# A hybrid decoder step with 64 experts: the expert loop put into program order

## The chip, the cores and the metric

The kernel runs on one core of one Trainium2 chip. The metric is the device time of one execution in microseconds. The median of three runs of the kernel before is 1366.9 us (1366.76 to 1370.61).

## The reference

One layer of a decoder is run for 512 prompt tokens and 8 sample tokens, 520 rows of 1024 features, in float32. A state-space branch and a windowed attention branch are merged and normalised; then comes the part that the change touches, a mixture of 64 experts with 8 chosen for each token, a shared expert, and a gated input of the layer:

```
scores = sigmoid(x @ w_router)                       # (520, 64)
top 8 of scores + bias; gates = top_s / sum * 2.5
for each expert e, for its tokens:  acc[tok] += gate * (silu(x[tok] @ w1[e]) * (x[tok] @ w3[e])) @ w2[e]
shared = (silu(x @ ws1) * (x @ ws3)) @ ws2
ple    = sigmoid(x @ w_ple_gate) * (p @ w_ple)
y      = layer_norm(2**0.25 * x + acc + shared + ple)
```

w1 and w3 are 1024 x 256 for each expert, w2 is 256 x 1024.

## The kernel before, in words

**Numbers.** Every float32 operand of a large product is cut in two parts, `hi` (a rounded copy that ScalarE, ACT, writes) and `lo` (the rest, by a subtraction on VectorE, DVE, or GpSimd, POOL). TensorE (PE) then adds three products: hi by hi, lo by hi, hi by lo. `split` (line 267) issues both instructions. All weights are read from HBM as pieces of 128 x 1024 float32, 512 KB, and split on the chip.

**The stream of weights.** `Stream` (line 288) holds the list of pieces in the order in which they are used: for round e of the expert loop four pieces of w1 and w3 of expert e (A), then two pieces of w2 of expert e-1 (B). `get(n)` first splits up to two pieces beyond n. Five buffers hold split pieces; seven (at the start more) hold raw pieces. When a piece has been split, its raw buffer is free and the next load is given to the SyncE queue (SP). One split in six, that with `m % 6 == 2`, has its subtraction on POOL.

**The expert loop** (line 1599) has 65 rounds. The experts are sorted by their number of tokens, and `CAPS` gives the number of rows of each, from 112 to 56. Round e does:

- `expert_in(e)`: 24 matmuls of 512 columns with the turned rows of expert e, SiLU on ACT (line 1254), the product `hg` on DVE.
- `turn(e+1)`: eight transposes of the gathered rows `xg` of the next expert, in two PSUM banks, each split into `xgh` and `xgl`.
- `expert_out(e-1)`: 12 matmuls; ACT weighs the result with the gate into `y` (line 1450, two buffers), and POOL issues an indirect DMA that adds `y` to the rows of a sum in HBM (line 1451, the scatter). Two sums take turns up to expert 49, then all go to the first.
- `ffn_turn(e)`: two transposes of `hg`, split into `hh` and `hl`, which expert_out(e) needs in the next round.
- `fetch(e+3)`: the search for the rows of a later expert (`find`, line 1383): DVE compares places (`one_hot`), PE adds five small bf16 matmuls, DVE reduces them to `idx`; then POOL issues an indirect DMA that gathers the rows (line 1414), in three buffers.

**Side work** is spread over the rounds: the second half of the shared expert (`shared_more`), its output (`shared_out`), the layer input in four column groups (`layer_inputs`), the scales of the last norm, and the addition of the second sum to the rows (`second_sums`, on POOL). Each group begins with `side_weights`, which loads two or three pieces through one raw buffer and splits them in two to three splits at once. All side products use one PSUM buffer (`psx`), and so does the search from expert 3 on. Pieces are handed out by a quota, 44 over 55 rounds.

**The order.** Instructions are put in order by a scheduler of the framework, which estimates durations and may move an instruction ahead of others of its engine. `T.pinned` keeps PE's instructions in program order in the part before the loop and is False in the loop (line 1590); DVE, ACT and POOL are never pinned. On the chip each engine runs its instructions in the order so fixed, and waits at each for its data.

Of the kernel before, what the change touches and what calls it, by code (L numbers as in the profile page):

```python
# [18 lines left out]
F32 = mybir.dt.float32  # L19
# [9 lines left out]
NT = 520  # L29
# [18 lines left out]
YB = 2  # L48
PRE = 5
VB = 5  # L50
N_SIDE = 44
SECOND = 50
SIDE = N_SIDE / 55
N_DENSE = 54
assert len(CAPS) == NE

# [143 lines left out]
@with_exitstack  # L200
def trunk_step(ctx: ExitStack, tc: tile.TileContext, I, O):
    nc = tc.nc
    V, S, G = nc.vector, nc.scalar, nc.gpsimd

    class Tensor:

# [81 lines left out]
    class Stream:  # L288
# [34 lines left out]
        def split_to(self, n):  # L323
            while self.done < min(n, len(self.srcs)):
                p, tag, bufs = self.pools(self.done, 1)
                if p is None:
                    return
                self.load_to(self.done + 1)
                raw, was = self.raw.pop(self.done)
                hi = p.tile([128, 1024], F32R, tag=tag + "h", bufs=bufs, name="hi")  # L330
                lo = p.tile([128, 1024], F32R, tag=tag + "l", bufs=bufs, name="lo")
                m = self.done - P2 - 2
                split(hi, lo, raw, G if 0 < m < 6 * (NE - 1) and m % 6 == 2 else V)
                self.parts[self.done] = (hi, lo)
                self.done += 1
                self.held[was] -= 1
                self.load_to(self.done + 40)
# [957 lines left out]

    def shared_more(i):

        if i < 0:
            side_weights(lambda a, b: wd[50 + a // 1024], 2048)
            H['ph'], H['pl'] = (H[k][:, 0:2048].rearrange("p (k n) -> p k n", k=8) for k in ('ph', 'pl'))  # L1300
            return
        out = psx.tile([128, 512], F32, tag="x", name="x")[0:TT, 0:256]
        whole(shared_product(out, i, H['ph'], H['pl'], range(8)))
        shared_turn(shared_mid(out, moe.tile([MAX_CAP, 256], F32, tag="hg", bufs=2, name="sg")[0:TT, 0:128]), i, 1)

    def side_weights(src, n):

        H['ph'] = pw.tile([128, 2560], F32R, tag="ph", name="ph")
        H['pl'] = pw.tile([128, 2560], F32R, tag="pl", name="pl")
        for a in range(0, n, 1024):  # L1310
            b = min(a + 1024, n)
            raw = pw.tile([128, 1024], F32, tag="praw", name="praw")
            nc.sync.dma_start(raw[:, 0:b - a], src(a, b))
            split(H['ph'][:, a:b], H['pl'][:, a:b], raw[:, 0:b - a])

    def shared_out(i):

        if i < 0:
            side_weights(lambda a, b: wd[52 + a // 1024], 2048)
            H['ph'], H['pl'] = (H[k][:, 0:2048].rearrange("p (h k n) -> p h k n", h=2, k=2) for k in ('ph', 'pl'))  # L1320
            return
        hh, hl = H['shared'][:, i, 0], H['shared'][:, i, 1]
        for h in range(2):
            ps = psx.tile([128, 512], F32, tag="x", name="x")[0:TT]
            n = 0
            for k in range(2):
                for l, w in ((hh, H['ph']), (hh, H['pl']), (hl, H['ph'])):
                    T.matmul(ps, lhsT=l[:, k], rhs=w[:, h, k], start=(n == 0), stop=(n == 5))
                    n += 1
            v = H['x1'][:, i, 512 * h:512 * h + 512]  # L1330
            V.scalar_tensor_tensor(v, v, ALPHA, ps, op0=ALU.mult, op1=ALU.add)
        if i == 4:
            pT = py.tile([128, 2, NT], F32, tag="y", bufs=YB, name="pT")
            nc.sync.dma_start(pT, I['pT'])
            both = py.tile([128, 2, 2, NT], F32R, tag="side", name="pTs")
            H['pTh'], H['pTl'] = both[:, 0], both[:, 1]
            split(H['pTh'], H['pTl'], pT)

    def layer_inputs(q, i):

        if i < 0:
            side_weights(lambda a, b: I['wp'][q, :, a:b], 2560)
            H['ph'], H['pl'] = (H[k].rearrange("p (k n) -> p k n", k=10) for k in ('ph', 'pl'))
            return
        c = slice(TT * i, TT * i + TT)
        ps = psx.tile([128, 512], F32, tag="x", name="x")
        for o, xs, k0, kn in ((ps[0:TT, 256:512], (H['pTh'], H['pTl']), 0, 2), (ps[0:TT, 0:256], (H['xh'], H['xl']), 2, 8)):
            n = 0
            for k in range(kn):
                for l, w in ((xs[0], H['ph']), (xs[0], H['pl']), (xs[1], H['ph'])):  # L1350
# [20 lines left out]

    def second_sums(i):

        t = pw.tile([128, 1024], F32, tag="praw", name="second")[0:TT]
        nc.sync.dma_start(t, sumsD[1][TT * i:TT * i + TT])
        add(G, H['x1'][:, i], H['x1'][:, i], t)


    XG, XT, HG, HT, GC, IX = {}, {}, {}, {}, {}, {}

    OH = {}

    def find(e, what=(0, 1)):

        m = CAPS[e]
        if e not in OH:
            OH[e] = one_hot(e, m)
        a, b = what[0], what[-1] + 1
        ps = psx.tile([128, 512], F32, tag="x", name="x") if e > 2 else bank()
        for i in R5:  # L1390
            T.matmul(ps[0:m, 3 * a:3 * b], lhsT=OH[e][:, i], rhs=H['what'][:, i, 3 * a:3 * b, e], start=(i == 0), stop=(i == 4))
        both = moe.tile([128, 2], F32, tag="gc", bufs=8, name="both")
        V.tensor_reduce(both[0:m, a:b], ps[0:m, 3 * a:3 * b].rearrange("p (w n) -> p w n", n=3), axis=AX.X, op=ALU.add)
# [13 lines left out]

    def fetch(e):
        find(e)
        gather(e)  # L1410

    def gather(e):
        m = CAPS[e]
        G.indirect_dma_start(out=XG[e % 3][0:m], out_offset=None, in_=xD[:, :],  # L1414
                             in_offset=bass.IndirectOffsetOnAxis(ap=IX[e][0:m, 0:1], axis=0),
                             bounds_check=NT - 1, oob_is_err=False)

    def turn(e):
        x, m = XG[e % 3], CAPS[e]
# [17 lines left out]
    def expert_out(e):  # L1437
# [8 lines left out]
        if e >= NE - 2:  # L1446
# [4 lines left out]
        G.indirect_dma_start(out=sumsD[e % 2 if e < SECOND else 0][:, :], out_offset=bass.IndirectOffsetOnAxis(ap=IX.pop(e)[0:m, 0:1], axis=0),  # L1451
                             in_=y, in_offset=None, compute_op=ALU.add)

    def kept(e, ps):

# [21 lines left out]
    def second_phase():  # L1477
# [116 lines left out]
        fill(1000)  # L1594
        close_pool(disp)
        py = open_pool("py")
        side = [(q, i) for q in range(-2, 4) for i in range(-1, 5)]
        side += [(4, -1), (4, 0), (4, 1)] + [(5, i) for i in R5]
        for e in range(NE + 1):
            if e == NE - 1:  # L1600
                last_rows()
# [3 lines left out]
                turn(e + 1)  # L1605
            if e:
                expert_out(e - 1)
            else:
                H['shared'] = py.tile([128, 5, 2, 2, TT], F32R, tag="side", name="st")
                mids = py.tile([MAX_CAP, 1024], F32, tag="y", bufs=YB, name="mids")  # L1610
                mids = [shared_mid(H['first half'][i], mids[0:TT, 128 * i:128 * i + 128]) for i in R5]
            if 0 < e < 6:
                shared_turn(mids[e - 1], e - 1, 0)
            if 0 < e < NE - 1:
                HT[e] = ffn_turn(HG.pop(e), CAPS[e])
            if e + 3 < NE:
                fetch(e + 3)
            if e == 4:
                close_pool(pre)
                pw = open_pool("pw")  # L1620
            while side and (e - 4) * SIDE >= N_SIDE - len(side) + 1:
                q, i = side.pop(0)
                if q == -2:
                    shared_more(i)
                elif q == -1:
                    shared_out(i)
                elif q < 4:
                    layer_inputs(q, i)
                elif q == 5:
                    second_sums(i)  # L1630
                else:
                    last_scales(i)
        assert not side
        acc = {}
        for i in R5:
# [142 lines left out]
    def whole(g):  # L1778
        for _ in g:
            pass  # L1780
# [71 lines left out]
```

## Time and profile before

| | |
|---|---|
| median of 3 runs | 1366.9 us |
| profiled execution | 1371.03 us |
| its span, first to last instruction | 1369.2 us |
| mean granted clock of TensorE | 0.928 |
| PE busy | 1191.9 us, 87% |
| DVE busy | 970.3 us, 71% |
| ACT busy | 700.3 us, 51% |
| POOL busy | 560.2 us, 41% |
| HBM read and written | 276.32 MB and 32.87 MB |

The shares are of the span. Everything after this is read from stretches of the span, with times in microseconds from its start. A busy time of PE holds the modelled ends of its matmuls, which overlap. SiLU number e, the only instruction of line 1254, marks the end of expert_in(e), so the time between two of them is a round.

### The profile page before, as it was taken

To read this page: it belongs to the slowest core of one execution; us is meant where nothing else is said; L and a number is where in the kernel's file an instruction comes from. 1 tells how busy PE (TensorE), PEld (TensorE's weight loads), DVE (VectorE), ACT (ScalarE), POOL (GpSimd) and SP (SyncE) were. 2 spreads that over 40 slices of the span, in tenths; PEclk is the share of its full clock that TensorE was granted. 3 is DMA by queue.
4 is the path that set the end of the run, shared out by engine and by line. 5 is a ranking of instruction groups with operands and counts; after the bars stand their busy time and mean duration, and the time that the engine had idled before them with its cause. 6 is when DMAs were issued, how large, how long until landed. Compare 5 with 4: busy or idle time off the path is not lost. (4 is left out here: it accounts for less than half of the span.)

```text
span 1369.2 us, 20382 instructions
## 1 busy us (share of the span) xinstructions
PE 1191.9 (87%) x7082; PEld 890.2 (65%) x7084; DVE 970.3 (71%) x1397; ACT 700.3 (51%) x1055; POOL 560.2 (41%) x327
## 2 busy tenths in 40 slices
PE   7699899999997979787899688899999998968783
PEld 7699799999877756565566466576666664434441
DVE  7873748633588877576788578789789777647656
ACT  4131534222213766566567456767567665546562
POOL 1821231010124436243565354465664644464326
PEclk9898899999997989898999899999999999788896
DMA  7476553442512989798899798999999899887773
GB/s 286 134 240 120 191 182 105 118 116 92 191 60 89 294 222 314 226 286 262 257 319 319 224 274 275 310 306 305 303 300 321 288 301 266 224 229 243 260 191 100
DMA packets 114182, 312.93 MB, mean 229 GB/s; under 512 B 36986, under 2 KB 37410, under 8 KB 113000
## 3 DMA queue, kind: packets, MB, share of 16 engines
q1 hardware_dynamic: 68892, 249.24, 54.2%
q0 software_dynamic: 30208, 41.20, 14.0%
q10 hardware_dynamic: 14974, 21.14, 5.9%
q8 instruction: 57, 0.93, 0.3%
q14 instruction: 51, 0.42, 0.1%
HBM read 276.32 MB, written 32.87 MB: 226 GB/s over the span
## 5 line engine op out<-in xcount | busy, mean ns | idle before, releaser
L265 DVE TENSOR_TENSOR lo<-raw,hi 128x1024 fp32r<-128x1024 f32 x371 | 552.6, 1503 | 170.1 <-ACT hi L269 166.0
L269 ACT ACTIVATE hi<-raw 128x1024 fp32r<-128x1024 f32 x434 | 450.9, 1056 | 253.4 <-DMA raw<-in_we_dram 80.0
L1451 POOL DMA_INDIRECT accD<-y,idx x62 | 137.0, 2210 | 267.2 <-ACT hh L269 118.2
L210 PE MATMUL a<-hi,xgh 128*64 128x512 f32 (+18 forms) x512 | 211.8, 414 | 8.8 <-DVE xgl L265 6.0
L210 PE MATMUL a<-lo,xgh 128*64 128x512 f32 (+18 forms) x512 | 210.1, 410 | 7.3 <-DVE lo L265 7.3
L210 PE MATMUL a<-hi,xgl 128*64 128x512 f32 (+18 forms) x512 | 206.9, 404 | 0.0
L265 POOL TENSOR_TENSOR lo<-raw,hi 128x1024 fp32r<-128x1024 f32 x63 | 169.3, 2687 | 46.6 <-ACT hi L269 34.8
L1414 POOL DMA_INDIRECT xg<-xD,idx x64 | 125.0, 1953 | 146.5 <-DVE idx L1396 105.1
L210 PE MATMUL mm<-xh,hi 128*128 128x260 f32 (+1 forms) x576 | 121.7, 293 | 19.1 <-DVE r L259 10.7
L210 PE MATMUL mm<-xl,hi 128*128 128x260 f32 (+1 forms) x576 | 120.2, 291 | 0.8 <-DVE xl L265 0.8
L210 PE MATMUL mm<-xh,lo 128*128 128x260 f32 (+1 forms) x576 | 120.5, 291 | 0.0
L210 PEld LDWEIGHTS a<-hi,xgh 128*64 128x64 f32 (+18 forms) x512 | 75.7, 148 | 53.3 <-DVE xgl L265 7.6
L210 PEld LDWEIGHTS a<-lo,xgh 128*64 128x64 f32 (+18 forms) x512 | 75.6, 148 | 48.4 <-DVE lo L265 11.6
L210 PEld LDWEIGHTS mm<-xh,hi 128*128 128x128 f32 x576 | 92.8, 197 | 20.1 <-issue 11.0
L210 PE MATMUL mm<-lo,hh 128*64 128x512 f32 (+18 forms) x256 | 88.3, 428 | 18.3 <-POOL lo L265 17.8
L210 PEld LDWEIGHTS a<-hi,xgl 128*64 128x64 f32 (+18 forms) x512 | 75.5, 147 | 41.1 <-issue 4.0
L215 PE MATMUL a<-ident,xg 64*128 64x64 f32 (+18 forms) x512 | 57.7, 243 | 46.8 <-DMA xg<-xD,idx 38.5
L215 PEld LDWEIGHTS a<-ident,xg 64*128 64x128 f32 (+18 forms) x512 | 49.6, 148 | 73.0 <-DMA xg<-xD,idx 26.4
L210 PE MATMUL mm<-hi,hh 128*64 128x512 f32 (+18 forms) x256 | 88.0, 425 | 8.8 <-ACT hh L269 8.8
L1450 ACT ACTIVATE y<-mm,both 78x1024 f32<-78x1024 f32 (+19 forms) x62 | 68.8, 1109 | 52.1 <-PE mm L210 35.4
L210 PEld LDWEIGHTS mm<-xl,hi 128*128 128x128 f32 x576 | 92.2, 195 | 1.3 <-DVE xl L265 1.1
L210 PEld LDWEIGHTS mm<-xh,lo 128*128 128x128 f32 x576 | 92.4, 195 | 0.1
(410 smaller groups left out, 1999.1 us busy)
## 6 DMA issues: line engine op xcount, KB each, us to landing
raw<-in_we_dram SPq DMA_DIRECT2D x384, 512.0 KB
raw<-in_wd_dram SPq DMA_DIRECT2D x50, 512.0 KB
accD<-zeros_b POOLq DMA_DIRECT2D x2, 2560.0 KB
praw<-in_wp_dram SPq DMA_DIRECT2D x8, 512.0 KB
base<-in_xtok_dram ACTq DMA_DIRECT2D x1, 2080.0 KB
xD<-base ACTq DMA_DIRECT2D x5, 416.0 KB
second<-accD SPq DMA_DIRECT2D x5, 416.0 KB
acc<-accD SPq DMA_DIRECT2D x5, 416.0 KB
```

Of the source, the lines that this page charges most:

```text
L210: ins = nc.tensor.matmul(*a, **k)
L215: ins = nc.tensor.transpose(*a, **k)
L265: return e.tensor_tensor(out=o, in0=a, in1=b, op=ALU.subtract)
L269: a = S.activation(hi, src, AF.Copy)
L1414: G.indirect_dma_start(out=XG[e % 3][0:m], out_offset=None, in_=xD[:, :], in_offset=bass.IndirectOffsetOnAxis(ap=IX[e][0:m, 0:1], axis=0), ...
L1450: S.activation(y.rearrange("p (h n) -> p h n", h=2), ps[0:m], AF.Copy, scale=GC.pop(e)[0:m])
L1451: G.indirect_dma_start(out=sumsD[e % 2 if e < SECOND else 0][:, :], out_offset=bass.IndirectOffsetOnAxis(ap=IX.pop(e)[0:m, 0:1], axis=0), ...
```

## The change

In the expert loop the instructions of PE, DVE and ACT are marked to stay in program order, and so are gathers and scatters on POOL. `V` and `S` become wrappers that mark what they issue while `pinned` is True:

```diff
-    V, S, G = nc.vector, nc.scalar, nc.gpsimd
+    G = nc.gpsimd
+    class InOrder:
+        pinned = False
...
+            def run(*a, **k):
+                ins = call(*a, **k)
+                if self.pinned:
+                    tc.keep_in_program_order(ins)
+                return ins
+    V, S = InOrder(nc.vector), InOrder(nc.scalar)
```

All splits of weights have their subtraction on DVE, and the second sums are added there:

```diff
-                m = self.done - P2 - 2
-                split(hi, lo, raw, G if 0 < m < 6 * (NE - 1) and m % 6 == 2 else V)
+                split(hi, lo, raw)
...
-        add(G, H['x1'][:, i], H['x1'][:, i], t)
+        add(V, H['x1'][:, i], H['x1'][:, i], H['raw'])
```

The search takes a PSUM buffer of `psa2` (three, shared with expert_in, turn and the small transposes) for every expert:

```diff
-        ps = psx.tile([128, 512], F32, tag="x", name="x") if e > 2 else bank()
+        ps = bank()
```

The side work becomes a list of 55 pieces, each a load and a work. A weight split is a piece of its own. Each round from the fifth on does the work of one piece and then issues the load of the next:

```diff
+    def side_work():
+        groups = [(2, lambda c: wd[50 + c], shared_more), (2, lambda c: wd[52 + c], shared_out)]
+        for q in range(4):
+            groups.append((3, lambda c, q=q: I['wp'][q, :, 1024 * c:min(1024 * c + 1024, 2560)], lambda i, q=q: layer_inputs(q, i)))
+        for n, (parts, src, piece) in enumerate(groups):
+            for c in range(parts):
+                yield (lambda c=c, src=src: side_load(src(c))), (lambda c=c: side_weights(1024 * c))
+            for i in R5:
+                yield None, (lambda i=i, piece=piece: piece(i))
+            if n == 1:
+                yield side_tokens_load, side_tokens
+        for i in range(-1, 2):
+            yield None, (lambda i=i: last_scales(i))
+        for i in R5:
+            yield (lambda i=i: side_load(sumsD[1][TT * i:TT * i + TT])), (lambda i=i: second_sums(i))
```

`side_load` gives a load of 512 KB or less into the one raw buffer to SP; `side_weights` splits what it holds; `side_tokens_load` and `side_tokens` load and split the token features of the layer input, in one of the two `y` buffers. The loop becomes:

```diff
         for e in range(NE + 1):
...
                 turn(e + 1)
             if e:
                 expert_out(e - 1)
+            for n in (3, 4) if e == 0 else (e + 4,):
+                if n < NE:
+                    fetch(n)
+            if e - 1 in YE:
+                scatter(e - 1)
...
-            if 0 < e < NE - 1:
-                HT[e] = ffn_turn(HG.pop(e), CAPS[e])
-            if e + 3 < NE:
-                fetch(e + 3)
...
-            while side and (e - 4) * SIDE >= N_SIDE - len(side) + 1:
...
+            if e > 4 and side:
+                side.pop(0)[1]()
+            if e > 3 and side and side[0][0]:
+                side[0][0]()
+            if 0 < e < NE - 1:
+                HT[e] = ffn_turn(HG.pop(e), CAPS[e])
```

So the gather of a round is for expert e+4 instead of e+3 and stands ahead of the scatter on POOL, and ffn_turn stands behind the side piece.

## Rows read from the trace of the kernel before

**Rows 1.** Windows: us, busy time and count by engine, clock, DMA share, GB/s.
```profile
456.00:1343.00 887.00, 763.76 (x4059) 499.41 (x4057) 663.34 (x844) 551.65 (x764) 430.99 (x199) 0.93 0.89 272
860.00:980.00 120.00, 111.70 (x664) 77.81 (x663) 97.20 (x125) 81.21 (x113) 66.47 (x30) 0.98 0.97 307
```

**Rows 2.** Timeline: start, us, engine, line, tiles: SiLU 5, 60, 63; the closing matmuls.
```profile
521.87 0.38 ACT L1254 ACTIVATE hg<-a 92x256 f32<-92x256 f32 x1 [0.34 <-PE a L210]
...
1281.05 0.38 ACT L1254 ACTIVATE hg<-a 56x256 f32<-56x256 f32 x1 [0.67 <-PE a L210]
...
1328.10 0.38 ACT L1254 ACTIVATE hg<-a 56x256 f32<-56x256 f32 x1 [0.55 <-PE a L210]
...
1343.75 2.01 PE L210 MATMUL mm<-yy,to 128*104 128x512 f32 x4 [5.60 <-PEq L1645]
```

**Rows 3.** Waits of PE, 456 to 1343: us in total, times, longest.
```profile
PE a L215 <- DMA xg<-xD,idx: 38.1, 8, 9.7
```

**Rows 4.** Groups of splits, 456 to 1343: count, busy us, mean ns.
```profile
L265 DVE TENSOR_TENSOR lo<-raw,hi 128x1024 fp32r<-128x1024 f32 x318 | 479.8, 1524 | 113.2 <-ACT hi L269 109.2 <-issue 1.9
...
L265 POOL TENSOR_TENSOR lo<-raw,hi 128x1024 fp32r<-128x1024 f32 x62 | 166.9, 2692 | 46.5 <-ACT hi L269 34.8 <-issue 11.0
```

**Rows 5.** Timeline: splits on DVE with and without POOL beside them.
```profile
1234.31 3.49 DVE L265 TENSOR_TENSOR lo<-raw,hi 128x1024 fp32r<-128x1024 f32 x3
...
1238.67 2.42 POOL L262 TENSOR_TENSOR base<-base,second 104x1024 f32<-104x1024 f32 x1
...
1239.06 5.44 DVE L265 TENSOR_TENSOR lo<-raw,hi 128x1024 fp32r<-128x1024 f32 x1 [0.49 <-ACT hi L269]
```

**Rows 6.** Timeline: from the end of one expert_in to the split of the next rows.
```profile
1065.49 0.39 PE L210 MATMUL a<-hi,xgl 128*64 128x512 f32 x1
1065.72 0.61 PE L210 MATMUL mm<-hi,hh 128*66 128x512 f32 x2
1065.91 0.38 ACT L1254 ACTIVATE hg<-a 64x256 f32<-64x256 f32 x1 [3.66 <-PE a L210]
...
1066.26 0.71 PE L215 MATMUL a<-ident,xg 64*128 64x64 f32 x8
1066.33 0.41 DVE L259 TENSOR_TENSOR hg<-hg,a 64x256 f32<-64x256 f32 x1 [2.39 <-ACT hg L1254]
1067.23 0.64 ACT L269 ACTIVATE xgh<-a 128x256 fp32r<-128x256 f32 x2
```

**Rows 7.** Timeline: side matmuls, search, small transposes, one-hot, hi splits.
```profile
1039.89 0.28 PE L210 MATMUL x<-ph,x1h 128*104 128x256 f32 x1
...
1040.01 0.28 PE L210 MATMUL x<-pl,x1h 128*104 128x256 f32 x1
...
1046.49 0.33 PE L210 MATMUL x<-what,oh 104*64 104x6 bf16 x5
...
1046.74 0.34 PE L215 MATMUL a<-ident,hg 66*128 66x66 f32 x2
...
1046.89 0.42 PE L210 MATMUL a<-hi,xgh 128*66 128x512 f32 x1
...
1048.83 0.47 DVE L1404 TENSOR_TENSOR oh<-pc,place 104x320 bf16<-104x320 f32 x1
...
1058.35 3.90 ACT L269 ACTIVATE hi<-raw 128x1024 fp32r<-128x1024 f32 x4
```

**Rows 8.** Windows (columns as rows 1) behind two waits of PE.
```profile
1184.60:1191.30 6.70, 5.68 (x15) 3.04 (x16) 4.90 (x9) 3.22 (x4) 3.78 (x3) 0.50 0.98 284
1066.50:1073.00 6.50, 4.43 (x26) 2.60 (x25) 5.88 (x7) 4.81 (x8) 2.49 (x3) 1.00 0.72 179
```

**Rows 9.** Timeline: the wait of PE ahead of the first of those windows.
```profile
1184.62 0.47 PE L215 MATMUL a<-ident,hg 62*128 62x62 f32 x2 [1.26 <-DVE hg L259]
```

**Rows 10.** Tile y: the scatter on POOL (ns min/median/max), and its landing.
```profile
L1451 POOL DMA_INDIRECT accD<-y,idx x62: 1432/2014/4824, 471.9 to 1324.4; - x62
...
DMA to landing us min/median/max: 6.6/11.8/21.4
```

More of the change, by code (lines that the diff above doesn't have):

```diff
@@ L50 @@
 VB = 5
-N_SIDE = 44
 SECOND = 50
-SIDE = N_SIDE / 55
 N_DENSE = 54
@@ L202, in trunk_step, with __init__, __getattr__ @@
     nc = tc.nc
-    V, S, G = nc.vector, nc.scalar, nc.gpsimd
+    G = nc.gpsimd
+    class InOrder:
+        pinned = False
+        def __init__(self, engine):
+            self.engine = engine
+        def __getattr__(self, name):
+            call = getattr(self.engine, name)
+            def run(*a, **k):
[3 more added lines that the diff above has]
+                return ins
+            return run
+    V, S = InOrder(nc.vector), InOrder(nc.scalar)
     class Tensor:
@@ L1296, in shared_more, with side_load, side_weights @@
     def shared_more(i):
[L1298 to L1301, printed above, removed]
+        ph, pl = (t[:, 0:2048].rearrange("p (k n) -> p k n", k=8) for t in H['side'])
         out = psx.tile([128, 512], F32, tag="x", name="x")[0:TT, 0:256]
-        whole(shared_product(out, i, H['ph'], H['pl'], range(8)))
+        whole(shared_product(out, i, ph, pl, range(8)))
         shared_turn(shared_mid(out, moe.tile([MAX_CAP, 256], F32, tag="hg", bufs=2, name="sg")[0:TT, 0:128]), i, 1)
[L1306 to L1314, printed above, removed]
+    def side_load(src):
+        H['raw'] = pw.tile([128, 1024], F32, tag="praw", name="praw")[0:src.shape[0], 0:src.shape[1]]
+        nc.sync.dma_start(H['raw'], src)
+    def side_weights(a):
+        if a == 0:
+            H['side'] = [pw.tile([128, 2560], F32R, tag=nm, name=nm) for nm in ("ph", "pl")]
+        raw = H['raw']
+        split(*(t[:, a:a + raw.shape[1]] for t in H['side']), raw)
     def shared_out(i):
[L1318 to L1321, printed above, removed]
+        ph, pl = (t[:, 0:2048].rearrange("p (h k n) -> p h k n", h=2, k=2) for t in H['side'])
         hh, hl = H['shared'][:, i, 0], H['shared'][:, i, 1]
@@ L1326, in shared_out @@
             for k in range(2):
-                for l, w in ((hh, H['ph']), (hh, H['pl']), (hl, H['ph'])):
+                for l, w in ((hh, ph), (hh, pl), (hl, ph)):
                     T.matmul(ps, lhsT=l[:, k], rhs=w[:, h, k], start=(n == 0), stop=(n == 5))
@@ L1331, in shared_out, with side_tokens, side_tokens_load @@
             V.scalar_tensor_tensor(v, v, ALPHA, ps, op0=ALU.mult, op1=ALU.add)
[L1332 to L1337, printed above, removed]
+    def side_tokens():
+        both = py.tile([128, 2, 2, NT], F32R, tag="side", name="pTs")
+        H['pTh'], H['pTl'] = both[:, 0], both[:, 1]
+        split(H['pTh'], H['pTl'], H.pop('pT'))
+    def side_tokens_load():
+        H['pT'] = py.tile([128, 2, NT], F32, tag="y", bufs=YB, name="pT")
+        nc.sync.dma_start(H['pT'], I['pT'])
     def layer_inputs(q, i):
[L1341 to L1344, printed above, removed]
+        ph, pl = (t.rearrange("p (k n) -> p k n", k=10) for t in H['side'])
         c = slice(TT * i, TT * i + TT)
@@ L1349, in layer_inputs @@
             for k in range(kn):
-                for l, w in ((xs[0], H['ph']), (xs[0], H['pl']), (xs[1], H['ph'])):
+                for l, w in ((xs[0], ph), (xs[0], pl), (xs[1], ph)):
                     T.matmul(o, lhsT=l[:, k, c], rhs=w[:, k0 + k], start=(n == 0), stop=(n == 3 * kn - 1))
@@ L1372, in second_sums @@
     def second_sums(i):
-        t = pw.tile([128, 1024], F32, tag="praw", name="second")[0:TT]
-        nc.sync.dma_start(t, sumsD[1][TT * i:TT * i + TT])
-        add(G, H['x1'][:, i], H['x1'][:, i], t)
+        add(V, H['x1'][:, i], H['x1'][:, i], H['raw'])
[14 more added lines that the diff above has]
+            yield (lambda i=i: side_load(sumsD[1][TT * i:TT * i + TT])), (lambda i=i: second_sums(i))
     XG, XT, HG, HT, GC, IX = {}, {}, {}, {}, {}, {}
-    OH = {}
+    OH, YE = {}, {}
     def find(e, what=(0, 1)):
@@ L1409, in fetch @@
         find(e)
-        gather(e)
+        tc.keep_in_program_order(gather(e))
     def gather(e):
         m = CAPS[e]
-        G.indirect_dma_start(out=XG[e % 3][0:m], out_offset=None, in_=xD[:, :],
-                             in_offset=bass.IndirectOffsetOnAxis(ap=IX[e][0:m, 0:1], axis=0),
-                             bounds_check=NT - 1, oob_is_err=False)
+        return G.indirect_dma_start(out=XG[e % 3][0:m], out_offset=None, in_=xD[:, :],
+                                    in_offset=bass.IndirectOffsetOnAxis(ap=IX[e][0:m, 0:1], axis=0),
+                                    bounds_check=NT - 1, oob_is_err=False)
     def turn(e):
@@ L1450, in expert_out, with scatter @@
         S.activation(y.rearrange("p (h n) -> p h n", h=2), ps[0:m], AF.Copy, scale=GC.pop(e)[0:m])
-        G.indirect_dma_start(out=sumsD[e % 2 if e < SECOND else 0][:, :], out_offset=bass.IndirectOffsetOnAxis(ap=IX.pop(e)[0:m, 0:1], axis=0),
-                             in_=y, in_offset=None, compute_op=ALU.add)
+        YE[e] = y
+    def scatter(e):
+        y, m = YE.pop(e), CAPS[e]
+        sums = sumsD[e % 2 if e < SECOND else 0]
+        tc.keep_in_program_order(G.indirect_dma_start(
+            out=sums[:, :], out_offset=bass.IndirectOffsetOnAxis(ap=IX.pop(e)[0:m, 0:1], axis=0),
+            in_=y, in_offset=None, compute_op=ALU.add))
     def kept(e, ps):
@@ L1596, in second_phase @@
         py = open_pool("py")
-        side = [(q, i) for q in range(-2, 4) for i in range(-1, 5)]
-        side += [(4, -1), (4, 0), (4, 1)] + [(5, i) for i in R5]
+        side = list(side_work())
+        T.pinned = V.pinned = S.pinned = True
         for e in range(NE + 1):
@@ L1607, in second_phase @@
                 expert_out(e - 1)
-            else:
+            for n in (3, 4) if e == 0 else (e + 4,):
[3 more added lines that the diff above has]
+                scatter(e - 1)
+            if e == 0:
                 H['shared'] = py.tile([128, 5, 2, 2, TT], F32R, tag="side", name="st")
@@ L1620, in second_phase @@
                 pw = open_pool("pw")
-            while side and (e - 4) * SIDE >= N_SIDE - len(side) + 1:
[L1622 to L1632, printed above, removed]
+            if e > 4 and side:
[4 more added lines that the diff above has]
+                HT[e] = ffn_turn(HG.pop(e), CAPS[e])
+        T.pinned = V.pinned = S.pinned = False
         assert not side
```

## Prediction

> **What bounds the kernel now.** I read the windows first, then the waits, then the order of time inside single rounds. Everything that changes lies in the expert loop, from about 456 us to 1343.8 us, where the closing matmuls start [rows 1, 2]. There no engine is full: TensorE (PE) is busy 764 of 887 us at a mean granted clock of 0.93, VectorE (DVE) 663, ScalarE (ACT) 552, and the DMA engines 0.89 [rows 1]. The reader should see two loads near the length of the loop. The first is DMA: 887 us at 272 GB/s are 241 MB, and in the best long stretch (share 0.97) 307 GB/s flowed [rows 1], so these bytes need 786 us, 12.3 us in each of 64 rounds. The second is PE: 887 - 764 = 123 us idle, and a mean clock of 0.93 means about 124 us at the lower of its two levels, half of that lost, so that unbroken full-clock work would be some 710 us. Between 710 or 786 and 887 lies what order alone can win. The largest single wait of PE is for the gathered rows of an expert: 38.1 us in 8 waits [rows 3]. The gathers come late because POOL works in order, and a gather stands behind DVE splits given to POOL and behind scatters.
>
> **The change, part by part.**
>
> *Splits leave POOL.* 62 splits of 2.69 us go from POOL to DVE [rows 4]. On DVE three in a row took 3.49 us, 1.16 each [rows 5], so DVE gains 62 x 1.16 = 72 us. But DVE's 318 splits now average 1.524 us, because POOL's elementwise work stops DVE: one split took 5.44 us beside an addition of 2.42 us on POOL [rows 5]. Without that they lose 318 x 0.36 = 115 us. The five additions of second sums also go to DVE, the same width as a split, 5 x 1.16 = 6 us. DVE's load falls by about 37 us; nothing on the path is priced by it directly, since DVE is not full; what counts is its place in the round.
>
> *Program order: the round's timetable.* Program order decides who waits for whom, so I lay out one round with 0 at the moment when PE has issued the last matmul of expert_in. Matmuls of 512 columns follow each other by 0.23 us (1065.49 to 1065.72) [rows 6]: 24 of expert_in 5.55, 12 of expert_out 2.8. The eight transposes of turn take 0.71 [rows 6], the search 0.25 (1046.49 to 1046.74), the two transposes of ffn_turn 0.15 until the next matmul (1046.74 to 1046.89) [rows 7]; with the change of kind I take 0.2. PE alone would need 5.55 + 0.7 + 2.8 + 0.25 + 0.2 = 9.5.
> ACT: SiLU starts at 0.19 and ends at 0.57; xgh twice, 0.64 together, ends at 1.3 [rows 6]; then come the two hi splits of the next expert's first weights, 3.90/4 = 0.98 each [rows 7], ending at 2.3 and 3.3; then y.
> DVE: the product hg starts at 0.61 and takes 0.41 [rows 6]; the xgl halves lie before 2.3; the two lo splits end at 2.3 + 1.16 = 3.5 and 4.7; only then, since find stands behind expert_out in the program, comes the one-hot compare, 0.47 [rows 7], ending at 5.2.
> PE has issued turn and expert_out at 0.7 + 2.8 = 3.5 and the search needs the one-hot: a new wait of 1.7 us in each round with a search. The next expert_in starts at 5.2 + 0.25 + 0.2 = 5.65 and ends at 11.2; with hops between engines I take 11.3. DVE then splits from about 7 us on, four times 1.16, and ends near 11.7, in time for the next product at 11.9. Queued behind the waiting search on PE are the side piece, ffn_turn and the whole next expert_in; behind the one-hot on DVE the index for the gather. Bounds of this wait: 0, if the compare gets through early; 3 us, if it stands behind a split whose weights have not landed. I keep 1.7, the value of the rows.
> A piece of layer inputs is 30 matmuls of 256 columns at 0.12 (1039.89 to 1040.01) [rows 7], 3.5 us: such a round takes 14.8. A shared piece is 2.8 us of matmuls and about 1 us of waiting for SiLU and product, or for the one PSUM buffer: 15.1. The round of a weight split stays at 11.5, since its split stands in the gap and its data were asked for a round earlier.
>
> *The sum.* Rounds 5 to 59 carry 55 pieces: 20 x 14.8 = 296; 10 x 15.1 = 151; 16 weight rounds x 11.5 = 184; the token features 12; three pieces of scales and five second sums at 13, 104. Together 747 us, against 759 from SiLU 5 to SiLU 60 before [rows 2]. DMA does not set it: eight rounds of one layer-inputs group take 5 x 14.8 + 3 x 11.5 = 108 us, and DMA needs 8 x 12.3 = 98. The start, 66 us up to SiLU 5, I leave as it is: a gather wait goes, but the first rounds' order is stricter. The end, 62.7 us from SiLU 60, has no searches: three rounds at DMA's 12.3 and the 15.7 us from SiLU 63 on as now, 53 [rows 2]. So 66 + 747 + 53 = 866 before the clock. Before, the granted clock fell after a wait of 1.26 us and stayed at 0.50 for 6.7 us, but it held at 1.00 through 6.5 us of which PE was idle for 2.1 [rows 8, 9]. A fall of that length costs 3.35 us. The new waits are about as long as the first, the falls after long gather waits go, so I add four falls, 13 us: 879, against 887.8. That is 9 us less than the profiled execution's own 1371.0 (its span of 1369.2 and 1.8 around it); it ran 4.1 us above the median of 1366.9, so 1358 is the forecast for the median.
>
> *Smaller parts.* Gathers a round earlier and ahead of the scatter: the 38 us of waits [rows 3] go, and what is late next is the one-hot; this is in the timetable. The search in the banks of expert_in, turn and ffn_turn instead of the side buffer: it takes the bank that the product frees at 1.0, four microseconds before; nothing, and if DVE slipped by more than that, the wait would be the same as that for the one-hot. Side data loaded a round ahead: a load stands in SP's queue behind the weights and has a round of 11 us; nothing, at worst the wait of one landing in each of 22 loads, 2 us each. The token load takes one of two y buffers and waits for a scatter's landing, 11.8 us in the median [rows 10], about a round: 0 to 10 us once; I take 0.
>
> **Rivals.**
> A. DMA's pace. If the compare is early enough, the loop runs at the pace of the bytes: 786 us and some 20 for start and end, 806, 82 less: 1285. For it: 120 us at share 0.97 already now [rows 1]. Against: the timetable has DMA waiting in 30 of 55 rounds.
> B. Slower: the clock. The new wait comes in every round in the same place, between expert_out and the side piece or the next expert_in. If the clock falls in a quarter of the 55 rounds, 14 x 3.35 = 47 us instead of 13: 1392. It decides from seven falls on, (9 + 13)/3.35. For it: 0.50 after only 1.26 us; against: 1.00 through 2.1 us of idleness [rows 8, 9]. The Trainium skill (TensorE: Matmul & The Clock Gate, HAM oscillation) describes a loop that waits in each tile and falls back to the slow clock each time. By that all 55 rounds would fall, an estimate of 171 us more; the two gaps of the trace bear it out only in part.
> C. POOL and the scatters. From expert 50 on all scatters add into one buffer, each behind the last one's landing, 11.8 us in the median and 21.4 at most; POOL's part of a scatter goes from 1.4 to 4.8 us, 2.0 in the median [rows 10]; should DVE's added splits push each to the longest, 12 rounds with 2.8 more are 34 us: 1392. Against: the same chain stands there before. The Trainium skill (SBUF — State Buffer, Who interferes with whom) holds, as an inference, that a two-input vector operation does not keep GpSimd from writing descriptors. By that this rival costs nothing, and the spread of POOL's times would have another cause.
>
> **How the numbers follow.** The forecast has 0.60, with its own range of 1337 to 1375 (the wait in the search between 1.3 and 2.0 us). A has 0.10, B 0.22, C 0.08. A measurement here tells about 0.3%, 4 us, from no change. Of the forecast's 0.60 some 0.39 lie below 1362.8, 0.13 within, 0.08 above. Faster 0.39 + 0.10 = 0.49, same 0.13, slower 0.08 + 0.22 + 0.08 = 0.38. The range reaches past B and C and more than halfway to A: 1314 to 1398.
>
> **What would show it.** Right: PE's largest wait in the loop is that of the search's weight load for the one-hot, some 55 times about 1.7 us; hardly a wait for gathered rows; splits on DVE at 1.2 us; rounds of 11 and 15 us. Wrong: no such wait and DMA at 0.97 (A); a clock under 0.9 through the middle of the loop (B); gaps at y or at the gathers after expert 50 (C).

## The result: 4% slower, and the profile after

The changed kernel takes 1425.2 us (median, 1419.8 to 1434.1) against 1368.7 for the kernel before on the same chip: ratio 1.0419, 95% interval [1.0355, 1.0484]. The forecast was 1358, its range ended at 1398. The profiled execution took 1419.8 us with a span of 1418.0 and a mean granted clock of 0.922.

The loop's milestones, from the timeline of the kernel after (start, us, engine, line, tiles; SiLU 5, 60 and 63, then the closing matmuls, as in [rows 2]):

```profile
522.66 0.38 ACT L214 ACTIVATE hg<-a 92x256 f32<-92x256 f32 x1 [1.68 <-PE a L228]
...
1333.90 0.38 ACT L214 ACTIVATE hg<-a 56x256 f32<-56x256 f32 x1 [2.28 <-PE a L228]
...
1377.05 0.38 ACT L214 ACTIVATE hg<-a 56x256 f32<-56x256 f32 x1 [1.43 <-PE a L228]
...
1390.52 0.72 PE L228 MATMUL last<-yy,to 128*104 128x512 f32 x1 [5.15 <-PEq L1676]
```

SiLU 5 to SiLU 60 took 811.2 us, before 759.2. SiLU 5 came 0.8 us later, and from SiLU 60 to the closing matmuls it took 56.6 us instead of 62.7. So the loss lies in rounds 5 to 59. Three stretches of them by the windows (columns as in [rows 1]): all of them, 6.7 us around a late compare, and the best long one:

```profile
522.66:1333.90 811.24, 679.13 (x3601) 447.58 (x3599) 553.36 (x799) 471.91 (x658) 184.67 (x110) 0.92 0.84 264
566.30:573.00 6.70, 3.84 (x21) 3.84 (x22) 2.10 (x4) 2.04 (x2) 1.75 (x2) 0.50 0.64 195
924.90:1028.50 103.60, 91.29 (x551) 62.53 (x549) 78.12 (x117) 67.80 (x96) 28.52 (x16) 1.00 0.90 288
```

The DMA engines were less busy (0.84; 0.91 before in the same rounds), DVE and POOL had more room than before. Nobody is full; everybody waits. The waits, by engine (who waits for whom: us in total, times, longest), whole span:

```profile
PE a L228 <- DVE oh L214: 121.1, 62, 6.6
PE a L228 <- ACT hi L214: 18.0, 3, 9.3
...
ACT hi L214 <- DMA raw<-in_we_dram: 47.9, 43, 3.4
ACT y L214 <- DMA accD<-y,idx: 41.7, 7, 11.0
...
SPq L336 <- DVE lo L214: 782.5, 356, 25.2
```

PE's wait for gathered rows, 38.1 us in [rows 3], has vanished; the search's wait for the one-hot compare stands in its place, three times as large. The groups of instructions that answer to [rows 4] (count, busy us, mean ns, then the idle time before them):

```profile
L214 DVE TENSOR_TENSOR lo<-raw,hi 128x1024 fp32r<-128x1024 f32 x434 | 519.6, 1240 | 136.0 <-ACT hi L214 128.9 <-DMA raw<-in_we_dram 5.7
...
L1443 POOL DMA_INDIRECT xg<-xD,idx x64 | 82.4, 1288 | 638.9 <-issue 485.3 <-PE a L233 118.4 <-DVE oh L214 17.6
```

Splits went from a mean of 1.52 to 1.24 us, as forecast. A gather's issue holds POOL for 1.29 us in the mean (1.95 before).

What a bad round is made of shows in the timeline of the kernel after at three places: an ordinary late compare (903 to 906 us), a very late one (566 to 569), and a late y (519 to 540):

```profile
519.66 2.38 POOL L1485 DMA_INDIRECT accD<-y,idx  x1 [0.30 <-DVE lo L214]
...
536.68 1.11 ACT L214 ACTIVATE y<-mm,both 94x1024 f32<-94x1024 f32 x1 [11.00 <-DMA accD<-y,idx]
...
538.98 3.90 ACT L214 ACTIVATE hi<-raw 128x1024 fp32r<-128x1024 f32 x4
...
540.09 0.73 PE L228 MATMUL a<-hi,xgh 128*88 128x512 f32 x1 [7.14 <-ACT hi L214]
...
566.28 1.06 ACT L214 ACTIVATE hi<-raw 128x1024 fp32r<-128x1024 f32 x1 [1.79 <-DMA raw<-in_we_dram]
...
567.37 1.23 DVE L214 TENSOR_TENSOR lo<-raw,hi 128x1024 fp32r<-128x1024 f32 x1 [1.62 <-ACT hi L214]
568.51 0.59 DVE L214 TENSOR_TENSOR oh<-pc,place 104x420 bf16<-104x420 f32 x1
569.16 0.53 PE L228 MATMUL a<-what,oh 104*84 104x6 bf16 x5 [6.63 <-DVE oh L214]
...
902.77 1.21 DVE L214 TENSOR_TENSOR lo<-raw,hi 128x1024 fp32r<-128x1024 f32 x1
903.22 1.06 ACT L214 ACTIVATE hi<-raw 128x1024 fp32r<-128x1024 f32 x1 [0.88 <-DMA raw<-in_we_dram]
...
904.31 1.22 DVE L214 TENSOR_TENSOR lo<-raw,hi 128x1024 fp32r<-128x1024 f32 x1 [0.33 <-ACT hi L214]
905.45 0.52 DVE L214 TENSOR_TENSOR oh<-pc,place 104x350 bf16<-104x350 f32 x1
906.02 0.34 PE L228 MATMUL a<-what,oh 104*70 104x6 bf16 x5 [3.03 <-DVE oh L214]
```

At 902.77 and 904.31 DVE makes the two splits, and only then the compare, which depends on neither. The second split waits for ACT, ACT for weights that land 0.88 us late: the compare, the search, and on PE all that stands behind the search are late with them. At 566 the weights land later still and PE stands for 6.6 us; at 536 ACT holds four splits behind y, which has no buffer until a scatter issued 17 us earlier has landed.

### The profile page after: what moved, and what is told of

It is laid out like the page before. It is cut to its first block, busy times and chain, and to the rows that moved or that the text cites. A ratio compares the mean times of both kernels' runs of the same rounds, so it can differ in the third digit from the quotient of the medians.

```text
span 1418.0 us, 20397 instructions
## 1 busy us (share of the span) xinstructions
PE 1204.1 (85%) x7083; PEld 900.3 (63%) x7084; DVE 943.1 (67%) x1465; ACT 694.5 (49%) x1055; POOL 342.9 (24%) x259
## 3 DMA queue, kind: packets, MB, share of 16 engines
q1 hardware_dynamic: 68892, 249.24, 51.2%
q0 software_dynamic: 30208, 41.20, 13.6%
## 5 line engine op out<-in xcount | busy, mean ns | idle before, releaser
L214 DVE TENSOR_TENSOR lo<-raw,hi 128x1024 fp32r<-128x1024 f32 x434 | 519.6, 1240 | 136.0 <-ACT hi L214 128.9
L214 ACT ACTIVATE hi<-raw 128x1024 fp32r<-128x1024 f32 x434 | 435.6, 1056 | 175.7 <-PE mm L228 54.4
L1443 POOL DMA_INDIRECT xg<-xD,idx x64 | 82.4, 1288 | 638.9 <-issue 485.3
L228 PE MATMUL a<-hi,xgh 128*64 128x512 f32 (+18 forms) x512 | 218.2, 426 | 18.1 <-ACT hi L214 18.0
L228 PE MATMUL a<-hi,xgl 128*64 128x512 f32 (+18 forms) x512 | 213.2, 416 | 0.0
L1485 POOL DMA_INDIRECT accD<-y,idx x62 | 128.8, 2077 | 94.4 <-DMA accD<-y,idx 26.4
L228 PE MATMUL mm<-xh,hi 128*128 128x260 f32 (+1 forms) x576 | 121.2, 292 | 22.4 <-DVE r L214 12.5
L228 PE MATMUL a<-what,oh 104*64 104x6 bf16 (+18 forms) x335 | 24.2, 186 | 122.0 <-DVE oh L214 121.1
L228 PEld LDWEIGHTS <-oh 104*64 104x64 bf16 (+18 forms) x345 | 19.3, 122 | 152.2 <-DVE oh L214 149.6
L228 PE MATMUL mm<-lo,hh 128*64 128x512 f32 (+18 forms) x256 | 80.2, 394 | 1.7 <-DVE lo L214 1.7
L228 PE MATMUL mm<-hi,hl 128*64 128x512 f32 (+18 forms) x256 | 79.8, 393 | 0.0
```

The costliest lines, as they stand in the source:

```text
L214: ins = call(*a, **k)
L228: ins = nc.tensor.matmul(*a, **k)
L1443: return G.indirect_dma_start(out=XG[e % 3][0:m], out_offset=None, in_=xD[:, :], in_offset=bass.IndirectOffsetOnAxis(ap=IX[e][0:m, 0:1], a ...
L1485: tc.keep_in_program_order(G.indirect_dma_start(out=sums[:, :], out_offset=bass.IndirectOffsetOnAxis(ap=IX.pop(e)[0:m, 0:1], axis=0), in_= ...
```

## An account of the rounds

For each kernel I split the time from SiLU 5 to SiLU 60 into three: PE's idle time ahead of its instructions; what the half clock cost (half of the half-clock time in which PE was not idle); and the rest, PE's work at full clock. All are worked out from the profiled execution.

| kernel | SiLU 5 to 60 | PE idle | half-clock loss | rest | median, ratio to before [95%] |
|---|---|---|---|---|---|
| before | 759.2 | 95.3 | 29.8 | 634.0 | 1366.9 |
| after | 811.2 | 132.1 | 51.2 | 627.9 | 1425.2, 1.042 [1.036, 1.048] |
| e1 compare early | 764.1 | 92.5 | 32.5 | 639.0 | 1376.3, 1.009 [1.005, 1.012] |
| e2 shared turns early | 806.8 | 128.7 | 51.2 | 626.9 | 1419.6, 1.041 [1.033, 1.048] |
| e7 e1 and e2 | 758.5 | 90.5 | 30.0 | 637.9 | 1361.2, 0.997 [0.994, 1.000] |
| e13 e7, splits 3 ahead | 755.1 | 89.0 | 33.7 | 632.3 | 1357.2, 0.997 [0.994, 1.000] |
| e15 e13, compare first | 749.1 | 84.1 | 31.5 | 633.6 | 1349.3, 0.990 [0.985, 0.995] |
| e3 PE, POOL in order | 782.5 | 107.1 | 49.3 | 626.1 | 1401.8, 1.027 [1.017, 1.037] |
| e6 DVE, ACT, POOL in order | 824.1 | 123.1 | 70.7 | 630.4 | 1438.4, 1.052 [1.046, 1.057] |
| e4 no order | 727.9 | 69.1 | 23.5 | 635.3 | 1327.0, 0.973 [0.966, 0.980] |
| e10 e4, shared bank | 736.4 | 77.0 | 29.0 | 630.4 | 1351.6, 0.993 [0.991, 0.995] |
| e11 e4, old place of fetch | 752.0 | 102.6 | 20.7 | 628.7 | 1358.7, 0.996 [0.993, 0.999] |
| e14 e4, splits on POOL | 748.7 | 80.7 | 32.3 | 635.6 | 1364.5, 1.000 [0.997, 1.004] |
| e5 before, splits on DVE | 804.0 | 127.2 | 47.7 | 629.1 | 1410.0, 1.032 [1.025, 1.039] |
| e16 before, gather early, own bank | 746.0 | 84.6 | 26.7 | 634.7 | 1364.4, 1.000 [0.997, 1.003] |

The rest is 626 to 639 us in all kernels. No version does less work; they differ in how long PE stands still and in what the half clock costs.

## Experiments: is it the compare, or landings and buffers?

**e1: the compare made early, all else in program order.**
```
                 turn(e + 1)
+            if 0 < e and e + 4 < NE:
+                OH[e + 4] = one_hot(e + 4, CAPS[e + 4])
             if e:
                 expert_out(e - 1)
```


> Theory 1 (the compare): in program order the one-hot compare stands on DVE behind two splits of the next expert's weights, so PE waits at the search in every round, 121 us in all, longer where the weights land late, and the clock falls behind the long ones. With the compare issued right behind the turned rows that wait goes and rounds of layer inputs fall from 14.5 to about 13 us: 1425 becomes 1320 to 1360. Theory 2 (landings): the rounds are set by the landing of weights and scatters, and the compare is only where PE shows it. Then PE's wait moves to the hi and lo splits, and the time stays above 1400.

Measured 1376.3 us: 49 us of the 56 lost come back with one instruction moved. PE's largest waits in e1, 456 to 1345 us:

```profile
PE a L228 <- ACT hi L214: 49.9, 20, 8.4
PE a L228 <- DVE lo L214: 31.4, 38, 2.1
```

The wait for the compare in the loop is down from 120.0 to 6.0 us, but half of it has become waits for the next splits: what the compare hid behind itself. The compare is the larger cause, not the only one; the time falls between the two ranges.

**e2: all five turns of the first shared half in round 1**, so that their buffer, one of the two of y, is free from then on.
```
-            if 0 < e < 6:
-                shared_turn(mids[e - 1], e - 1, 0)
+            if e == 1:
+                for i in R5:
+                    shared_turn(mids[i], i, 0)
```


> The five products of the first shared half hold one of the two y buffers up to round 5, so y waits 11 us there for a scatter's landing, with all of ACT's later splits behind it. Here all five are turned in round 1 and the buffer is free from then on. Theory 1: 11 us and the round behind it are won, 1405 to 1415; the search waits stay near 120 us. Theory 2 (landings): the late weights of rounds 7 to 11 come from this stop, so those rounds get shorter too, 1385 to 1405.

Measured 1419.6, only 5.6 less and above both ranges; the intervals overlap. SiLU 5 to 6 fell from 23.6 to 12.0 us, but rounds 7, 8 and 11 still take 21.6, 19.7 and 19.4 with the compare late as before (122.2 us of waits, 62 times).

**e7: both edits.**

> The changed kernel, all in program order, with the compare of round e + 4 moved to just behind the turn of round e + 1 (1376 alone) and the five turns of the first shared half all in round 1 (1420 alone). If the two losses are separate and add: 1376 less 5.6 = 1368 to 1373. If the wait for y's buffer in round 5 was covered by the late compare and shows once that is gone: 1355 to 1367.

Measured 1361.2, in the second range, 15 us below e1: once the compare is early, y's wait is on the path. From 456 to 545 us y waits 19.5 us for scatters in e1 and 1.9 in e7, and SiLU 5 comes at 509.4 instead of 527.4 us, so most of this gain lies ahead of the stretch in the table. The changes don't add; one wait covered the other.

**e13: e7, and each weight block split three blocks ahead of its matmuls instead of two** (`def get(self, n, ahead=3)`).

> The changed kernel in program order with the compare early and the shared turns all in round 1 (1361), and each weight block split three blocks ahead of its matmuls instead of two. Theory J (what is left of the loss against 1327, 34 us, comes of splits just in time: they free the raw buffers late, loads start late, and TensorE waits 73 us for hi and lo): 1335 to 1350. Theory Q (a third split between product and compare only moves the wait, ACT and DVE stand in order behind a landing in either case): 1356 to 1375.

Measured 1357.2 (in the profile, 33 us of PE's waits are for the compare again: the third split stands ahead of it). Theory Q's range holds, and so does its mechanism.

**e15: e13, with the compare ahead of all splits of its round.**
```
+            if 0 < e and e + 4 < NE:
+                OH[e + 4] = one_hot(e + 4, CAPS[e + 4])
             if 0 < e < NE:
                 expert_in(e)
```


> The changed kernel in program order, shared turns in round 1, splits three blocks ahead (1357), and the compare of round e + 4 ahead of all splits of round e. Theory H (the rest of the order's loss is still the compare behind a split, 32 us of TensorE's idle time): 1325 to 1340. Theory W (the rest is weights that land late, with the splits and all that stands behind them in order): 1345 to 1360, the wait for the compare gone and that for hi grown.

Measured 1349.3, the best in program order, inside theory W's range. The waits of e15:

```profile
PE a L228 <- ACT hi L214: 34.7, 12, 9.4
PE a L228 <- DVE lo L214: 24.8, 30, 2.6
...
ACT hi L214 <- DMA raw<-in_we_dram: 102.7, 68, 5.4
...
ACT y L214 <- DMA accD<-y,idx: 44.9, 7, 12.3
```

The compare is gone from the list (3.6 us in all). What stays is splits whose weights have not landed, and y behind scatters, with all later splits of ACT behind it.

## Experiments: whose order costs?

**e4: nothing held in program order**, gathers and scatters included; side work, early gathers, own bank and splits as in the change.
```
-        T.pinned = V.pinned = S.pinned = True
+        pass
...
-        tc.keep_in_program_order(gather(e))
+        gather(e)
...
-        tc.keep_in_program_order(G.indirect_dma_start(
+        G.indirect_dma_start(
...
```


> No engine is in program order in the loop; all other parts of the change stay (splits on DVE alone, one side piece a round loaded a round ahead, the search in the shared banks, gather four ahead). If program order is the whole loss (theories 1 and 2 alike), the time is that of before or less, 1330 to 1375. If the other parts cost (DVE's 72 us of added splits, three banks for everything), it stays above 1390.

Measured 1327.0, below both ranges: program order costs 98 us, and the other parts of the change gain 40 against the kernel before. From 767 to 1263 us of e4 (windows):

```profile
767.00:1263.00 496.00, 458.48 (x2512) 293.23 (x2509) 369.23 (x541) 327.40 (x453) 138.92 (x76) 0.97 0.94 296
```

In the kernel after DMA flowed at 272 GB/s there. The timeline of e4 in one round shows the other order:

```profile
890.05 0.31 PE L228 MATMUL a<-what,oh 104*68 104x6 bf16 x5
...
891.06 0.50 DVE L214 TENSOR_TENSOR oh<-pc,place 104x340 bf16<-104x340 f32 x1
```

The search of one expert runs unhindered, and the compare after it is for a later one, placed between two splits.

**e3 and e6: one side of the order each.** e3 keeps PE and the gathers and scatters in order (`T.pinned = True` alone), e6 keeps DVE, ACT, gathers and scatters (`V.pinned = S.pinned = True`).

> Only PE, gathers and scatters keep program order in the loop; DVE and ACT are free for the scheduler again. Theory 1: the scheduler can put compare and product ahead of splits, the search wait falls below 40 us and the time to 1340 to 1390. Theory 2: the rounds stay as long, 1410 to 1430.

> The changed kernel with TensorE taken out of the program order; DVE, ACT and the gathers and scatters keep it. Theory C (the loss is made in DVE's and ACT's order: the one-hot compare behind two splits, y's scaling ahead of later splits; TensorE then only passes it on): 1390 to 1420 us, since the compare still comes as late as before, though TensorE may run a shared piece in that time. Theory P (TensorE's fixed order is what turns late operands into idle time): with other matmuls to run while the compare is late, 1330 to 1360.

e3 took 1401.8, between its ranges, and e6 1438.4: each alone is slow, and e6 came out 13 us above all four in order (1.052 against 1.042, intervals that just overlap). e3 lost the wait for the compare and got others; that DVE now serves its queue in another order than PE's is the likely reason, not shown by itself. The waits of e3 and of e6:

```profile
PE a L228 <- DVE hg L214: 29.6, 14, 6.0
PE a L233 <- DVE xgl L214: 20.6, 12, 4.4
PE a L233 <- DVE st L214: 18.7, 2, 9.5
PE a L233 <- DVE hl L214: 18.6, 7, 9.5
```

```profile
PE a L228 <- DVE oh L214: 88.7, 46, 5.5
```

So theory C holds for e6, beyond its range: with DVE and ACT fixed, a free PE still waits 88.7 us for the compare, and it stood at half clock for 150 us of rounds 5 to 59. That a part's cost is this engine's or that one's can't be said; orders must fit each other.

## Experiments: where do the 40 us come from?

**e5: the kernel before, its POOL splits on DVE** (`split(hi, lo, raw)` for the line that chose POOL).

> The kernel before with one edit: the 63 splits that ran on POOL run on DVE, all else as it was, in the scheduler's order. Theory S (the gain of some 40 us that the changed kernel keeps with nothing held in program order, 1327 against 1367, comes from POOL's splits alone: DVE's splits lose the neighbour that stretches them, 1.52 to 1.24 us in the mean): 1325 to 1340 us. Theory R (it comes from the rest: the work spread a piece a round and loaded a round ahead, the search in a bank of its own, the place of the gathers and scatters): 1355 to 1375, the split mean down to 1.3 us all the same.

Measured 1410.0: this part of the change alone is a loss of 43 us. The split's mean is 1.25 us, as hoped, but the view of waits of e5 shows the price:

```profile
PE a L215 <- DMA xg<-xD,idx: 87.4, 17, 13.5
```

It was 38.5 in the whole span before. Both theories fall. On POOL, where gathers and scatters take turns, the scatter now waits 242.9 us for ACT's y, 27 times (72.4 and 12 before), and a gather lands 12.5 us after its issue in the median instead of 8.8. Gathers stand behind that scatter in POOL's order; what lengthens the landing no run shows.

**e11: e4 with the search and gather at their old place**, expert e + 3 behind the scatter and the shared turn, instead of e + 4 ahead of them.
```
-            for n in (3, 4) if e == 0 else (e + 4,):
-                if n < NE:
-                    fetch(n)
...
+            if e + 3 < NE:
+                fetch(e + 3)
```


> The changed kernel with nothing held in program order (1327), but the search and gather of expert e + 3 behind the scatter and the shared turn of round e, as in the kernel before, instead of expert e + 4 ahead of that scatter. Theory F (the lead of the gather is the gain over 1410): 1370 to 1400, with waits for gathered rows of 50 us or more. Theory K (own bank) or spread side work: 1325 to 1340, the gathers in time all the same.

**e10: e4 with the search in the side work's single PSUM buffer again** (`ps = psx.tile(...) if e > 2 else bank()`).

> The changed kernel with nothing held in program order (1327), and the search from expert 3 on again in the side work's single PSUM buffer, as in the kernel before. That kernel with all splits on DVE takes 1410, 87 of its idle microseconds waiting for gathered rows. Theory K (the own bank is what lets the search and so the gather come early): 1380 to 1410, with TensorE waiting for gathered rows 60 us or more. Theory F (the gain lies in where the gather is issued and in the side work spread a piece a round): 1320 to 1335.

e11 took 1358.7, e10 1351.6: 32 and 25 us lost. The waits for gathered rows, first e11, then e10:

```profile
PE a L233 <- DMA xg<-xD,idx: 102.1, 20, 18.4
```

```profile
PE a L233 <- DMA xg<-xD,idx: 17.5, 5, 7.1
```

The gather's place is worth most, by the mechanism that theory F named (its range was too high); the bank is worth nearly as much, between the two ranges, and only a part of that is in the gather's wait.

**e14: e4 with the splits back on POOL. e16: the kernel before with the gather's new place and the own bank, splits still on POOL.**

> The changed kernel with nothing held in program order (1327) and the 63 splits back on POOL, as in the kernel before. Theory M (the move itself was a loss, hidden behind the earlier gather): 1290 to 1318 us. Theory N (the move costs only where it makes gathers late; beside it POOL's elementwise work stretches DVE's splits from 1.24 to 1.5 us): 1327 to 1345.

> The kernel before, splits on POOL and in the scheduler's order, with two things of the change: the search in the bank of expert_in and turn, and search and gather of expert e + 4 ahead of the scatter. If these two are the whole gain of the changed kernel without program order: 1320 to 1332 us, waits for gathered rows under 10 us. If the side work a piece a round and loaded ahead carries a part: 1335 to 1355.

1364.5 and 1364.4, both no different from before and above every range that I gave. The wait for gathered rows is under 1 us in both. In e14 PE waits for POOL's own splits instead, 42.6 us where it was 17.8 before; in e16 that wait stays at 16.7, and PE's idle time is spread over many others, 84.6 us between SiLU 5 and 60 against 95.3. The waits of e14:

```profile
PE mm L228 <- POOL lo L283: 42.6, 19, 7.3
```

This gives three corners of a square: splits moved alone, +43; gather early and own bank alone, 0; both, with the spread side work and the second sums on DVE, -40. With splits on POOL these last two make no difference (e14 against e16); with splits on DVE they were not left out. While POOL splits, an early gather only changes what PE waits for; while the gather is late, POOL's freedom is no use.

**e8 and e9: e4 further.** e8 has the shared turns in round 1 and both sums until expert 52 (`SECOND = 52`), e9 the compare of e1.

> The changed kernel with nothing held in program order (1327), the five turns of the first shared half in round 1, and both sums in use until expert 52 instead of 50. Theory L (the remaining long rounds 58 and 62 come of scatters that chain on one sum, and the early ones of the y buffer held through round 5): 1310 to 1322. Theory O (with a free order these waits are covered by other work): 1323 to 1331.

> The changed kernel with nothing held in program order (1327), and the compare of round e + 4 already behind the turn of round e + 1. If the scheduler places the compare by its place in the program, the waits for hg and xgl at the search (18 us) fall: 1310 to 1322. If it hoists the compare anyway: 1323 to 1331.

1330.2 (0.973 [0.968, 0.979]) and 1327.7 (0.975 [0.972, 0.979]): no different from e4, as theory O and the second case of e9 had it. Where the order is free, both faults are covered. e4 is the version to keep, 2.7% faster than before (interval 2.0 to 3.4%).

## Why the prediction was wrong, point by point

**Right.** The new wait: the search waits for the compare 62 times, 1.95 us in the mean where I had 1.7. In 44 of rounds 5 to 59 it waits 1.2 to 1.75 us. The splits' 1.24 us and the end of the gather waits came as forecast. So did the rounds in which nothing is late: for SiLU 31 to 39 and 44 to 52 the timetable gives 10 x 14.8 + 6 x 11.5 = 217 us; they took 104.8 + 107.8 = 212.6.

**The step that failed** is the sum of rounds 5 to 59, 747 + 13 = 760 for 811, in two of its terms. The smaller is the wait. With the 634 us of work that the account gives the kernel before, 747 holds 113 us of idle time; it was 132, 19 more. I bounded the wait by 3 us "if it stands behind a split whose weights have not landed" but kept the clean 1.7 for all rounds, 55 x 1.7 = 93.5 us. Measured are 110.6, because in eleven rounds it was 2.7 to 6.6 us, 44.7 in all. I also overlooked that the shared turns hold one of y's two buffers through round 5; PE's 7.1 us of waiting at 540 us come of that. The first seven rounds, 5 to 11, took 126.7 us, 28 above the timetable. In e2, without that buffer's wait, they still took 119.6, so the compare is the larger part of it.

**The larger term is the clock**: "I add four falls, 13 us" against 51 measured, in 23 half-clock stretches. The kernel before lost 29.8 us so between the same SiLUs, in 13 stretches, only five of them behind a gather's wait; the trace had it and I didn't count it. So a timetable at full clock was compared with a time that held these losses. At full clock rounds 5 to 59 had taken 759.2 - 29.8 = 729.4 us, and 747 is 18 us more: the forecast gain came of the clock's loss falling to 13 and of a shorter end, not of shorter rounds.

I wrote that the new waits are about as long as one that brought a fall, and took four falls for 55 rounds all the same. Twelve of the 23 stretches stand behind waits of 2.7 to 7.1 us, as at 566.3 us (the second window above). The other eleven, 24 us of the loss, stand behind waits for the compare of 1.2 to 1.7 us, the kind that I forecast. Rounds 16 and 17 are a pair with one kind of side piece, 66 matmuls and one wait (windows, then timeline):

```profile
707.12:724.68 17.56, 15.17 (x66) 9.50 (x65) 10.64 (x15) 8.35 (x12) 2.52 (x2) 0.81 0.67 209
724.68:739.51 14.83, 12.44 (x66) 7.99 (x65) 10.26 (x15) 8.21 (x12) 2.71 (x2) 1.00 0.84 261
...
712.01 0.35 PE L228 MATMUL a<-what,oh 104*78 104x6 bf16 x5 [1.61 <-DVE oh L214]
...
729.56 0.35 PE L228 MATMUL a<-what,oh 104*76 104x6 bf16 x5 [1.61 <-DVE oh L214]
```

The clock fell in the first and not in the second, and the round took 2.7 us longer. In the sixteen clean rounds, with waits of 1.3 to 1.6 us, it never fell. What decides between such rounds these rows don't show.

Rival B was close: 14 falls, 47 us instead of 13, where there were 51 us, in 22 of the 55 rounds. I gave it 0.22, and its 1392 lacked the idle time of the late rounds. The Trainium skill (TensorE: Matmul & The Clock Gate, HAM oscillation) describes a loop that waits some 3 to 5 us in each tile and whose clock drops each time. The trace agrees for the eleven late rounds, in all of which it fell. The prediction applied this to waits half as long; of the 44 rounds with those, eleven had a fall behind them.

A last 9.5 us of the miss are the choice of run: the forecast took 4.1 us off for the profiled execution of before, and that of after ran 5.4 below its own median.

**What the sum could not show**: that the change was two changes. Loose, its other parts gain 40 us; order takes 98. I put nothing on the path for "splits leave POOL", and e5 shows 43 us lost; I priced the search's bank at "nothing", and e10 shows 25 in the free order. DVE's load is not the price: e5 has the shorter splits that I forecast and waits for gathers. Rival C decided nothing: POOL's part of a scatter took 1.6 us in the median, 2.0 before, and after expert 50 y waited once for a landing, 10.8 us (before twice, 13.6). From SiLU 60 to the closing matmuls it took 56.6 us, forecast 53; what the 3.6 are made of was not taken apart.

**Still open.** Between e15 and e4 22 us remain. The waits say weights that land late and y; no run separates the two. That SP issues loads late because splits are tied to PE's pace (782.5 us of SP's waits are for splits) is argued, not shown; e13, which splits earlier, gained no measurable time. In e10 a part of the loss is unexplained. And where the order is free, an edit also lets the scheduler place other instructions anew. No run holds that order fixed, so what e5, e10, e11, e14 and e16 put down to a part of the change includes it.

## What to carry to other kernels

In a fixed order, look for instructions without inputs of their own round and put them ahead of what can wait for a landing: here one compare of 0.5 us, behind two splits, cost 49 us. When a timetable of a clean round comes out near the old time, price the rounds in which something lands late. Compare a timetable at full clock with the old time at full clock: count the half-clock stretches that the kernel already has before any is added or taken away. Take a change of several parts apart before judging one: here one part alone was worth nothing, another lost 43 us, and together, with the spread side work, they gained 40.

## What the runs showed of the hardware

- DVE's one-hot compare took 0.70 us in the mean with splits on POOL (e14) and 0.53 without (e4), and DVE's splits 1.48 against 1.24. The Trainium skill (SBUF — State Buffer, Who interferes with whom) says that a vector operation with two inputs in SBUF contends with a GpSimd instruction that reads it; the trace agrees. It also shows how much: in the kernel before, from 456 us on, 255 splits on DVE without an elementwise POOL instruction beside them took 1.22 us in the mean; 51 that had one beside them for over 0.5 us took 3.13, on average 1.08 more than the time they shared. So a split hardly advances meanwhile. The split of 5.44 us in [rows 5] had two such neighbours, the addition of 2.42 us and right behind it this one:

```profile
1241.03 2.37 POOL L265 TENSOR_TENSOR lo<-raw,hi 128x1024 fp32r<-128x1024 f32 x1
```

- Taking PE out of the order made more of it stand at half clock, not less: 150 us in rounds 5 to 59 of e6 against 123 in the kernel after.
- A scatter's landing took 4.4 us at least, 9.5 in the median and 34.4 at most after the change; before it was 6.6, 11.8 and 21.4 [rows 10].
